# A decoder trunk whose opening is rebuilt: c loaded by columns, the first norm by a ones matrix with Ln and Exp, the first input tile in full f32, and the whole order planned anew

## The chip, the core and the metric

One core of a Trainium2 chip. The metric is the device time of one execution in microseconds (us), as a median over runs; lower is better. The engines are TensorE (PE), VectorE (DVE), ScalarE (ACT), GpSimd (POOL) and SyncE (SP, which only issues DMAs here). They run their own instruction streams in order and meet at semaphores.

## The reference

Two layers on x of 512 tokens by 1024 features. Layer 0 mixes tokens with an RG-LRU block, layer 1 with gated linear attention; a gated FFN with a causal convolution follows each. Every sub-layer has an RMS norm before it, scaled and shifted by numbers that come from a conditioning vector c, and one behind it, gated the same way.

```python
c_act = silu(c)
for i in range(2):
    mod = c_act @ ada_w[i] + ada_b[i]          # 6 x 1024 numbers
    sh_m, sc_m, gt_m, sh_f, sc_f, gt_f = split(mod, 6)
    h = rmsnorm(x, norm_g[i, 0]) * (1 + sc_m) + sh_m
    y = rglru_mixer(h, ...) if i == 0 else gla_mixer(h, ...)
    x = x + gt_m * rmsnorm(y, norm_g[i, 1])
    h = rmsnorm(x, norm_g[i, 2]) * (1 + sc_f) + sh_f
    y = conv_ffn(h, ...)
    x = x + gt_f * rmsnorm(y, norm_g[i, 3])
```

In rglru_mixer the decay is exp(-8 r softplus(-lambda)), with r a sigmoid gate of the convolved input. All in float32.

## The kernel before

**Layout.** Activations lie with features on the 128 partitions and tokens along the free axis: x is 8 tiles of 128 x 512, in two token halves of 256. Weights come in units of 128 x 1024 f32 (`in_wall_dram`, 512 KB a load). Nearly all products are split: an operand is written as a high part in the fast format fp32r and a low part, the rest, and three matmuls replace one of full f32 (`mm3`, L804: high x high, high x low, low x high). A weight's high part is a cast on ScalarE (`acopy`, L601), its low part a subtraction on DVE (`tt`, L544). For the units that `BYLOAD` (L649) names, ScalarE writes the negated tile instead and a GpSimd DMA that adds (`accum`, L637) loads the weight a second time on top of it.

**Order.** The program text only records operations. `Sched.order` (L327) is a list scheduler with costs in us per operation, a model of the DMA queues and pool sizes (3 buffers for raw weights, 3 for `araw`, 8 for `w`); it runs through the program once and fixes the order on each engine. PE and SP keep the recorded order; DVE, ACT and POOL take the ready operation with the longest tail, nudged by random numbers with one seed per section of the program (`SEEDS`, L278; six sections).

**Opening.** c comes as one row (1 x 1024) and is spread over the partitions by two matmuls with a row of ones (L865); ScalarE's Silu takes it from PSUM into `cact`. x comes in four loads, two for each token half. For each half ScalarE squares 8 pieces, DVE adds them up to two tiles, PE sums them over the partitions with one column of ones (tokens land on partitions), ScalarE divides and adds epsilon, GpSimd raises to -0.5 (`pow`, L546), and PE spreads the result with an identity matmul (`rstd_from`, L831). The second half does this in bank 5 of the eight that hold the layer's first outputs. `idle` (L860) puts helper matmuls on a column of ones between these steps.

For each input tile k = 0..7 (L1346) two tiles of the ada weights come in (`ada_col`, L1330: scale, then shift; a DVE product with `cact` that sums along the row, 128 numbers each), and one weight unit ("rgx", k). DVE and ScalarE make h[k] = x[k] rstd (1 + sc) g + sh as high and low part (`h_tile`, L931), and PE adds its product into 8 banks for the 8 output tiles. Tile 0 goes by token halves: 8 matmuls for the high and 8 for the low part of each half, then 8 of 512 tokens with the weight's low part.

**What follows.** The convolution over the 8 outputs; gate projections and block gates (`gates`, L1426: three of four blocks with raw f32 weights), a softplus of lambda on 8 columns (L1382 to L1397, some twenty small DVE operations), Tanh, Exp, Sqrt and a scan (`recur`, L1445); FFN, attention with Ln and Exp in its norm (L1724), FFN. The tail is the last down projection, its norm and the stores.

## Time and profile before

| | |
|---|---|
| median of 3 runs | 1129.67 us (1124.52 to 1132.94) |
| profiled execution | 1127.41 us |
| its span, first to last instruction | 1125.6 us |
| instructions in the span | 14788 |
| HBM read, written | 217.82 MB, 6.31 MB |
| granted TensorE clock, mean | 0.998 |

The profile is of one execution. A table by stage gives for stretches of the span the busy time of PE, PE's weight loads, DVE, ACT and POOL with the number of their instructions, the granted clock, the share of the DMA engines and GB/s. A timeline row is: start, duration, engine, line, operation, output <- inputs by buffer names, shapes, how many in a row; in brackets the idle time before it and what ended it. The name `w` is both a pool of wide buffers and what lies in them, `g` and `gh` are 512- and 256-wide working tiles, `mm` and `nr` PSUM banks, `const` tiles that stay. Matmul rows overlap, so the distance between starts is the price of one, not the duration of a row. In the profile fp32r is written f32 on PE; a matmul of true f32 runs there as two passes, each a row of its own.

### The profile page before, as it was taken

What the parts mean: (1) busy time and instruction counts of PE and PEld (TensorE: products, weight loads), DVE (VectorE), ACT (ScalarE), POOL (GpSimd) and SP (SyncE); (2) the same over time, 40 slices, a digit from 0 to 9 for tenths busy, and PEclk for the clock granted to TensorE, in tenths of its full rate; (3) what the DMA queues carried; (4) which work ended last, traced back from release to release, by engine and by line L of the source; (5) the groups of instructions that cost most, each with busy time, mean ns of one, the idle gap of its engine ahead of it and who ended that gap; (6) DMA issues with size and microseconds to landing.
All of it is one profiled execution on the core that took longest, in us unless ns stands there. A gap on an engine that the chain in (4) does not pass through costs nothing.

```text
span 1125.6 us, 14788 instructions
## 1 busy us (share of the span) xinstructions
PE 1106.1 (98%) x5293; PEld 920.1 (82%) x5293; DVE 924.6 (82%) x1573; ACT 660.0 (59%) x1028; POOL 96.0 (9%) x124
## 2 busy tenths in 40 slices
PE   7999999999999999999999999999999999999997
PEld 6775879888888888788888888889888888888886
DVE  6989899877878878799969988856877787867888
ACT  5469948657446544555896855747556444453433
POOL 1001001011110111101110100002000000000000
PEclk9999999999999999999999999999999999999999
DMA  9889776699898998884461933327386766667542
GB/s 364 295 258 306 268 236 227 154 263 294 249 268 254 251 282 220 221 241 144 132 168 57 247 110 112 113 94 237 103 241 195 176 182 157 173 146 187 150 150 75
DMA packets 64907, 225.09 MB, mean 200 GB/s; under 512 B 7233, under 2 KB 7905, under 8 KB 64834
## 3 DMA queue, kind: packets, MB, share of 16 engines
q1 hardware_dynamic: 53314, 182.73, 46.5%
q0 software_dynamic: 11520, 41.42, 20.7%
q8 instruction: 42, 0.69, 0.2%
q14 instruction: 31, 0.25, 0.1%
HBM read 217.82 MB, written 6.31 MB: 199 GB/s over the span
## 4 chain that ended last, share of the span: by engine, by line
PE 64%; DMA 12%; DVE 9%; issue 7%; ACT 6%; POOL 1%; DVEq 0%; SPq 0%; POOLq 0%; ACTq 0%
PE mm L621 63%; DMA raw<-in_wall_dram 10%; ACT g L594 3%; DVE g L558 3%; DVE w L544 2%; ACT w L601 2%; DVE w L558 1%; DVE g L544 1%; DMA w<-in_adaT_dram 1%; DMA w<-in_wall_dram 1%; DVE araw L558 1%; ACT L594 1%; PE mm L628 1%; DVE const L544 1%; ACT w L594 1%
## 5 line engine op out<-in xcount | busy, mean ns | idle before, releaser
L621 PE MATMUL mm<-g,w 128*128 128x512 f32 (+2 forms) x2758 | 615.3, 381 | 4.1 <-DMA w<-in_wall_dram 2.3
L621 PEld LDWEIGHTS mm<-g,w 128*128 128x128 f32 (+1 forms) x2758 | 501.8, 188 | 104.8 <-DMA w<-in_wall_dram 2.7
L621 PE MATMUL mm<-w,g 128*128 128x512 f32 (+1 forms) x1428 | 330.4, 389 | 0.2 <-DVE w L544 0.2
L621 PEld LDWEIGHTS mm<-w,g 128*128 128x128 f32 x1428 | 265.4, 188 | 55.4 <-DVE w L544 0.6
L601 ACT CAST w<-raw 128x1024 fp32r<-128x1024 f32 x206 | 212.7, 1040 | 163.8 <-DMA raw<-in_wall_dram 134.8
L544 DVE TENSOR_TENSOR w<-raw,w 128x1024 fp32r<-128x1024 f32 x172 | 205.6, 1208 | 53.5 <-ACT w L601 51.2
L558 DVE SCALAR_TENSOR_TENSOR g<-mm,const,g 128x510 f32<-128x510 f32 (+3 forms) x199 | 147.5, 747 | 66.5 <-ACT g L594 63.9
L544 DVE TENSOR_TENSOR g<-g,g 128x256 f32<-128x256 f32 (+3 forms) x251 | 134.7, 563 | 21.1 <-ACT g L594 11.4
L594 ACT ACTIVATE g<-mm,const 128x512 f32<-128x512 f32 x115 | 86.1, 758 | 53.3 <-PE mm L621 51.3
L594 ACT ACTIVATE g<-g 128x512 f32<-128x512 f32 (+1 forms) x136 | 69.7, 543 | 46.3 <-DVE g L558 35.6
L558 DVE SCALAR_TENSOR_TENSOR araw<-araw,const 128x1024 f32<-128x1024 f32 x72 | 86.4, 1218 | 1.4 <-DMA araw<-in_adaT_dram 1.3
L601 ACT CAST g<-g 128x512 fp32r<-128x512 f32 (+2 forms) x84 | 50.2, 603 | 51.9 <-DVE g L544 50.8
L621 PE MATMUL mm<-g,g 128*128 128x256 f32 (+3 forms) x508 | 78.1, 309 | 0.8 <-DVE g L544 0.8
L621 PEld LDWEIGHTS mm<-g,g 128*128 128x128 f32 (+1 forms) x508 | 70.5, 191 | 6.2 <-DVE g L544 1.0
L637 POOL DMA_DIRECT2D raw<-in_wall_dram x46 | 39.8, 865 | 305.4 <-ACT raw L594 98.2
L637 POOL DMA_DIRECT2D w<-in_wall_dram x34 | 29.7, 873 | 353.9 <-ACT w L594 236.3
L544 DVE TENSOR_TENSOR const<-const,mm 128x512 f32<-128x512 f32 (+1 forms) x81 | 52.6, 674 | 4.6 <-PE mm L621 4.3
L594 ACT ACTIVATE w<-raw 128x1024 fp32r<-128x1024 f32 x34 | 36.0, 1058 | 13.9 <-DMA raw<-in_wall_dram 13.9
L594 ACT ACTIVATE g<-mm 128x512 f32<-128x512 f32 x44 | 26.1, 597 | 30.0 <-PE mm L621 16.5
L594 ACT ACTIVATE g<-const 128x512 f32<-128x512 f32 x47 | 29.0, 630 | 24.6 <-DVE const L544 11.7
L549 POOL TENSOR_TENSOR sm<-sm,const 128x1 f32<-128x1 f32 (+1 forms) x26 | 21.7, 834 | 229.2 <-DVE sm L558 205.2
L594 ACT ACT_TABLE_LOAD x29 | 37.2, 1283 | 3.0 <-DVE sm L569 1.8
(119 smaller groups left out, 747.3 us busy)
## 6 DMA issues: line engine op xcount, KB each, us to landing
raw<-in_wall_dram SPq DMA_DIRECT2D x218, 512.0 KB, 4.5
araw<-in_adaT_dram SPq DMA_DIRECT2D x72, 512.0 KB, 6.1
raw<-in_wall_dram POOLq DMA_DIRECT2D x44, 512.0 KB, 7.7
w<-in_wall_dram POOLq DMA_DIRECT2D x34, 512.0 KB, 8.4
w<-in_adaT_dram SPq DMA_DIRECT2D x24, 512.0 KB, 8.1
g<-dram SPq DMA_DIRECT2D x24, 256.0 KB, 5.7
dram<-const SPq DMA_DIRECT2D x8, 512.0 KB, 2.9
const<-in_xT_dram SPq DMA_DIRECT2D x4, 512.0 KB, 5.0
```

The source lines that it names most:

```text
L544: self.s.add(eng, dur, lambda: e.tensor_tensor(out.ap(), a.ap(), b.ap(), op=op), [a, b], [out])
L549: lambda: self.nc.gpsimd.tensor_tensor(out.ap(), a.ap(), b.ap(), op=ALU.pow), [a, b], [out])
L558: return self.nc.vector.scalar_tensor_tensor(out.ap(), a.ap(), f(sc), b.ap(), op0=op0, op1=op1, **kw)
L594: return self.nc.scalar.activation(out.ap(), a.ap(), func, **kw)
L601: self.s.add("act", (0.095 if self._sb(a) else 0.052) + out.n * 0.8325e-3, lambda: self.nc.scalar.copy(out.ap(), a.ap()), [a], [out], afte ...
L621: r.append(self.nc.tensor.matmul(g[0].ap(), g[1].ap(), g[2].ap(), start=g[3], stop=g[4], **kw))
L628: self.s.add("pe", 0.112, lambda: self.nc.tensor.transpose(out.ap(), a.ap(), ident.ap()), [a, ident], [out])
L637: self.s.add("pool", 0.9, lambda: self.nc.gpsimd.dma_start(out.ap(), src, accum_op=ALU.add), [out], [out], xfer=nbytes)
```

## The change

- c is loaded as 128 x 8 columns, and Silu is taken of these 8 columns; PE spreads each over the partitions by an identity matmul, and ScalarE copies the 1024 numbers out. The identity is loaded second, the parameters between the two halves of x.
- The first norm: squares and fewer DVE sums (2 in the first half, 1 in the second), then a full 128 x 128 matrix of ones on PE sums over partitions and spreads at once, in a bank of its own; ScalarE takes Ln and Exp(-0.5 ...). An explicit table load (natural log and exp in one set) stands ahead of the squares. `rstd_from` and `rstd_bcast` are gone.
- Input tile 0: its weight is kept as loaded, h tile 0 is kept in f32, and 16 matmuls of full f32 (8 for each token half) replace 32 + 8 split ones. Its high and low parts are made later, for the gate projections.
- Ada tiles of the shift part go to the pool `araw`, those of the scale part stay in `w`. Helper matmuls: `WARM` from (3, 2, 2, 2) to six ahead of all, then 0, 0, 2, 2.
- The softplus goes from DVE to GpSimd, its reciprocal by a power of -1.
- `BYLOAD` keeps only the odd units of the first up-projection: 9 of 18 make their low part on DVE now. ScalarE makes 9 negated copies fewer.
- Ln and Exp of the attention norm ask for the common table.
- The planner: new seeds in five of six sections, the cost of a GpSimd DMA 0.8 later when both queues are busy, PE warm at 7 us instead of 20.

```diff
-WARM_AT = 20.0
+HWR = 400e3
+WARM_AT = 7.0
-DMA_HW, DMA_SW = (393e3, 132e3, 1.63, 1.11, 0.34), (220e3, 123.5e3, 1.74, 1.85, 0.0)
+PRELOAD = {"lnexp": "natural_log_exp_and_others"}
+DMA_HW, DMA_SW = (HWR, 132e3, 1.63, 1.11, 0.34), (220e3, 123.5e3, 1.74, 1.85, 0.8)
...
-SEEDS, NUDGE = (9127, 7551, 2985, 6212, 7264, 540), 0.5
+SEEDS, NUDGE = (8506, 9486, 8142, 394, 6073, 540), 0.5
...
-BYLOAD = lambda what, *i: what in ('rgg', 'gv') or what == 'up' and i[0] == 0 and i[1] >= KF and 4 <= i[1] - KF
-WARM = (3, 2, 2, 2)
+BYLOAD = lambda what, *i: what in ('rgg', 'gv') or what == 'up' and i[0] == 0 and i[1] >= KF and 4 <= i[1] - KF and i[1] % 2
+WARM = (0, 0, 2, 2, 6)
+COLRING = "araw", "w"
+SQADD = 2, 1
...
-    e.load(crow[0:D].rows(1), c_d, 4096)
-    for j in range(4):
+    e.load(ccol[:], c_d, P * KD * 4)
+    e.load(ident[:], ident_d, P * P * 4)
+    for j in range(2):
         e.load(xbuf[j * D:(j + 1) * D], xT[:, j * D:(j + 1) * D], P * D * 4, alone=True)
     e.load(par[0:NPAR0], par_d[:, 0:NPAR0], P * NPAR0 * 4)
-    e.load(ident[:], ident_d, P * P * 4)
+    for j in range(2, 4):
+        e.load(xbuf[j * D:(j + 1) * D], xT[:, j * D:(j + 1) * D], P * D * 4, alone=True)
...
+            if UNITS[j][0] == ("rgx", 0):
+                raw = s.buf("w", F32, 2 * D)[0:D]
+                e.load(raw, wall[j, :, :n], P * n * 4, alone=True)
+                loaded[j] = raw
+                continue
...
+    e.act(csil[:], ccol[:], AF.Silu, table=("silu",))
+    e.act(warm[:], ones[0:1], AF.Exp, table=("lnexp",), after=s.last["act"])
+    lnexp = s.last["act"]
+    idle(4)
     for i in range(2):
         pc = xps[i]
-        e.mms([(pc[:], ones[0:P].rows(1), crow[i * S:(i + 1) * S].rows(1), True, True)])
-        e.act(cact[i * S:(i + 1) * S], pc[:], AF.Silu, table=("silu",))
+        e.mms([(pc[j * P:(j + 1) * P], csil[i * 4 + j:i * 4 + j + 1].map(lambda a: a.to_broadcast([P, P]), P),
+                ident[:], True, True) for j in range(4)])
+        e.acopy(cact[i * S:(i + 1) * S], pc[:])
+        idle(i)
...
+    def first_sums(i):
+
+        sq = squares[i]
+        for j in range(SQADD[i]):
+            e.tt(sq[2 * j][:], sq[2 * j][:], sq[2 * j + 1][:], ALU.add)
+        parts = [t[c:c + SH] for j, t in enumerate(sq) if j % 2 == 0 or j >= 2 * SQADD[i] for c in (0, SH)]
+        out = nrb[i * SH:(i + 1) * SH]
+        for j, v in enumerate(parts):
+            e.mms([(out, ones[:], v, j == 0, j == len(parts) - 1, True)])
+        r = rs0[i * SH:(i + 1) * SH]
+        e.act(r, out, AF.Ln, bias=epsc[0:1], scale=1.0 / D, table=("lnexp",), after=lnexp)
+        e.act(r, r, AF.Exp, scale=-0.5, table=("lnexp",))
...
+        h0 = gt()
+        for sl in HALVES:
+            e.stt(h0[sl], x[0][sl], mcol(0, 1, 0), rs0[sl], ALU.mult, ALU.mult)
+            e.act(h0[sl], h0[sl], AF.Identity, bias=mcol(0, 0, 0))
+            for m in range(NX):
+                e.mms([(xps[m][sl], w[m * P:(m + 1) * P], h0[sl], sl is HALVES[0], False, True)])
+        e.acopy(h[0][0][:], h0[:])
+        e.tt(h[0][1][:], h0[:], h[0][0][:].f32(), ALU.subtract)
...
-    e.dve(0.12, lambda: nc.vector.reciprocal(s8[:].ap(), s8[:].ap()), [s8[:]], [s8[:]])
-    e.tt(s8[:], s8[:], e8[:], ALU.mult)
+    e.pow(s8[:], s8[:], mone[:])
+    e.tt(s8[:], s8[:], e8[:], ALU.mult, "pool")
...
     for d in (13, 11, 9, 7, 5, 3, 1):
-        e.tt(p8[:], p8[:], q8[:], ALU.mult)
-        e.ts(p8[:], p8[:], 1.0 / d, None, ALU.add)
+        e.tt(p8[:], p8[:], q8[:], ALU.mult, "pool")
+        e.ts(p8[:], p8[:], 1.0 / d, None, ALU.add, eng="pool")
...
-        e.act(rs[:], sums[:], AF.Ln, bias=epsc[0:1], scale=1.0 / 256, table=("ln",))
-        e.act(rs[:], rs[:], AF.Exp, scale=-0.5, table=("exp",))
+        e.act(rs[:], sums[:], AF.Ln, bias=epsc[0:1], scale=1.0 / 256, table=("lnexp",))
+        e.act(rs[:], rs[:], AF.Exp, scale=-0.5, table=("lnexp",))
```

What the new order makes of it, at three places (numbers behind names tell buffers apart; lines of the changed file lie 4 to 12 further down).

PE before, from the spreading of the first half's norm (`nr_155`) on: `const_88` is the helper's operand, `w_192` the high part of the first weight, `g_203` the high part of h tile 0, `sm_210` the second half's norm.

```order
L621 MATMUL nr_155<-const_105,sm_175 128x128 x2
L621 MATMUL mm_168<-const_88 128x512 x2
L621 MATMUL mm_182<-const_84,gh_170 128x1 x2
L621 MATMUL mm_168<-const_88 128x512 x2
L621 MATMUL mm_109<-g_203,w_192 128x256
L621 MATMUL mm_119<-g_203,w_192 128x256
L621 MATMUL mm_219<-g_203,w_192 128x256
L621 MATMUL mm_182<-const_105,sm_210 128x128 x2
L621 MATMUL mm_168<-const_88 128x512 x2
L621 MATMUL mm_232<-g_203,w_192 128x256
```

PE now, from its first matmul on: `const_118` is Silu of c, `nr_163` the bank of the norm, `w_129` the weight as loaded.

```order
L626 MATMUL mm_98<-const_88 128x512 x6
L626 MATMUL mm_124<-const_103,const_118 128x128 x4
L626 MATMUL mm_141<-const_103,const_118 128x128 x4
L626 MATMUL nr_163<-g_137,const_84 128x256 x2
L626 MATMUL nr_163<-g_165,const_84 128x256 x2
L626 MATMUL mm_98<-const_88 128x512 x2
L626 MATMUL nr_163<-g_171,const_84 128x256 x2
L626 MATMUL nr_163<-g_177,const_84 128x256 x2
L626 MATMUL nr_163<-g_184,const_84 128x256 x2
L626 MATMUL mm_98<-const_88 128x512 x2
L626 MATMUL mm_124<-g_203,w_129 128x256
```

Both halves' norms now stand ahead of the first matmul of the layer, where the second half's stood in the middle of the tile, and six helpers stand ahead of everything.

DVE before, from the first product with an ada tile (`w_107`, scale; `w_111`, shift) to the second half of h tile 0; `w_115` and `w_123` are the ada tiles of input tile 1.

```order
L558 SCALAR_TENSOR_TENSOR w_107,const_179<-w_107,const_131 128x1024
L558 SCALAR_TENSOR_TENSOR w_111,const_179<-w_111,const_131 128x1024
L558 SCALAR_TENSOR_TENSOR gh_195<-const_98,const_186,nr_155 128x256
L569 TENSOR_SCALAR g_203<-gh_195,const_186 128x256
L558 SCALAR_TENSOR_TENSOR w_115,const_179<-w_115,const_131 128x1024
L558 SCALAR_TENSOR_TENSOR g_214<-gh_195,const_186,g_203 128x256
L544 TENSOR_TENSOR w_192<-raw_113,w_192 128x1024
L558 SCALAR_TENSOR_TENSOR gh_227<-const_98,const_186,mm_182 128x256
L558 SCALAR_TENSOR_TENSOR w_123,const_179<-w_123,const_131 128x1024
```

DVE now, from the same product (`w_116`, scale; `araw_122`, shift) to the last piece of input tile 1 (`g_249`); `g_182` is the norm, `g_203` h tile 0.

```order
L562 SCALAR_TENSOR_TENSOR w_116,const_187<-w_116,const_152 128x1024
L562 SCALAR_TENSOR_TENSOR const_193<-const_187,const_110,const_161 128x1
L562 SCALAR_TENSOR_TENSOR araw_122,const_187<-araw_122,const_152 128x1024
L562 SCALAR_TENSOR_TENSOR g_203<-const_106,const_193,g_182 128x256
L548 TENSOR_TENSOR const_193<-const_187,const_110 128x1
L562 SCALAR_TENSOR_TENSOR g_203<-const_106,const_193,g_182 128x256
L562 SCALAR_TENSOR_TENSOR w_131,const_187<-w_131,const_152 128x1024
L548 TENSOR_TENSOR g_219<-g_203,g_215 128x512
L562 SCALAR_TENSOR_TENSOR araw_135,const_187<-araw_135,const_152 128x1024
L562 SCALAR_TENSOR_TENSOR g_235<-const_106,const_193,g_182 128x512
L548 TENSOR_TENSOR w_223<-raw_133,w_223 128x1024
L562 SCALAR_TENSOR_TENSOR g_249<-g_235,const_193,g_242 128x512
```

The two columns of tile 0 are made on DVE, both halves of h follow each other, and the split of the first weight is gone.

POOL before, its first rows behind the memsets: the library load, the two powers of the first norm, the power of the softplus, the first accumulating DMA.

```order
L549 ISA
L549 TENSOR_TENSOR sm_175<-sm_172,const_90 128x2
L549 TENSOR_TENSOR sm_210<-sm_207,const_90 128x2
L549 TENSOR_TENSOR const_324<-const_92,const_321 128x8
L637 DMA w_499<-in_wall_dram 128x1024
```

POOL now, from the first accumulating DMA on (`w_451`, gate projection 0).

```order
L642 DMA w_451<-in_wall_dram 128x1024
L553 ISA
L553 TENSOR_TENSOR const_510<-const_90,const_504 128x8
L574 TENSOR_SCALAR const_522<-const_510 128x8
L553 TENSOR_TENSOR const_522<-const_522,const_92 128x8
L548 TENSOR_TENSOR const_522<-const_522,const_510 128x8
L548 TENSOR_TENSOR const_551<-const_522 128x8
L574 TENSOR_SCALAR const_553<-const_551 128x8
L548 TENSOR_TENSOR const_553<-const_553,const_551 128x8
```

The library load has moved behind the first DMA, and the softplus follows it: 23 small operations and two powers up to the two columns that Exp and Tanh read, with the DMA of gate projection 1 (`w_549`) after the tenth small one.

## The prediction, made before the changed kernel ran

> **What bounds the kernel now.** I read the page's busy table first, then the table by stage, then the timeline of the opening, engine by engine.

> ```profile
> PE 1106.1 (98%) x5293; PEld 920.1 (82%) x5293; DVE 924.6 (82%) x1573; ACT 660.0 (59%) x1028; POOL 96.0 (9%) x124
> 0.00:15.50 15.50, 10.37 (x31) 7.25 (x32) 8.07 (x17) 9.16 (x18) 1.50 (x9) 1.00 0.87 329
> ...
> 62.70:111.60 48.90, 47.80 (x170) 31.36 (x168) 44.76 (x76) 42.10 (x56) 4.47 (x7) 1.00 0.89 269
> ...
> 200.00:500.00 300.00, 297.72 (x1329) 247.16 (x1328) 241.36 (x377) 162.03 (x210) 35.44 (x41) 0.99 0.89 250
> 500.00:800.00 300.00, 297.46 (x1669) 256.96 (x1668) 248.25 (x492) 204.52 (x379) 24.59 (x35) 1.00 0.46 139
> ...
> 1100.00:1125.60 25.60, 19.24 (x97) 16.24 (x95) 21.13 (x43) 8.87 (x24) 0.00 (x0) 0.97 0.22 83
> ```

> In the stage rows the second number is PE's busy time. TensorE is the bound: out of a span of 1125.6 us it idles 19.5. Of these, 15.5 - 10.37 = 5.1 lie before the first matmul of the layer and 25.6 - 19.24 = 6.4 in the tail, which the change doesn't touch; 8.0 are left between. So whatever the new order does behind the opening, it can win at most 8.0 us. The opening is the other place: until 15.5 PE does nothing that the result needs but helpers, so an earlier first matmul is a gain in full.

> ```profile
> 8.87 1.86 PE L621 MATMUL nr<-const,gh 128*128 128x1 f32 x8 [2.85 <-DVE gh L544]
> 14.99 0.68 PE L621 MATMUL mm<-const 128*128 128x512 f32 x2
> 15.51 0.51 PE L621 MATMUL mm<-g,w 128*128 128x256 f32 x3
> 16.76 0.71 PE L621 MATMUL mm<-const,sm 128*128 128x128 f32 x4 [0.74 <-POOL sm L549]
> 18.54 0.50 PE L621 MATMUL mm<-g,w 128*128 128x256 f32 x2 [0.39 <-ACT g L601]
> 23.71 4.92 PE L621 MATMUL mm<-g,w 128*128 128x512 f32 x21
> 29.15 5.21 PE L621 MATMUL mm<-g,w 128*128 128x512 f32 x21
> 35.59 4.87 PE L621 MATMUL mm<-g,w 128*128 128x512 f32 x20 [0.28 <-DVE g L558]
> 62.73 5.60 PE L621 MATMUL mm<-g,w 128*128 128x512 f32 x24
> ```

> The first input tile (32 half-wide and 8 full matmuls) runs from 15.51 to 23.71 and is torn twice by the norm of the second token half: PE stands behind GpSimd's power (16.76) and behind ScalarE's copy out of the bank that the norm shares with an output (18.54). The later tiles take 29.15 - 23.71 = 5.44 us each; seven of them would take 38.1, and 62.73 - 23.71 = 39.0 pass, so 0.9 is lost there.

> **Opening: first matmul.** What feeds it:

> ```profile
> 8.07 0.75 DVE L544 TENSOR_TENSOR gh<-g 128x256 f32<-128x256 f32 x2
> 11.57 1.22 DVE L558 SCALAR_TENSOR_TENSOR w<-w,const 128x1024 f32<-128x1024 f32 x1
> 13.38 1.05 ACT L601 CAST w<-raw 128x1024 fp32r<-128x1024 f32 x1 [0.16 <-DMA raw<-in_wall_dram]
> 14.04 0.48 DVE L558 SCALAR_TENSOR_TENSOR gh<-const,const,nr 128x256 f32<-128x256 f32 x1
> 14.55 0.37 ACT L601 COPY g<-nr 128x256 f32<-128x256 f32 x1
> 15.94 1.05 ACT L601 CAST w<-raw 128x1024 fp32r<-128x1024 f32 x1 [0.52 <-DMA raw<-in_wall_dram]
> ```

> Two 512 KB loads lie between the casts at 13.38 and 15.94, so one takes 1.28. Counted back, the two ada tiles that x needs land at about 10.7 and 11.9, and the first weight at 13.2. The change keeps that order of bytes. It drops the weight's cast and the split of the first h half. DVE has 3 instead of 8 reductions of squares ahead of the ada products, so these no longer wait for DVE but for their loads: product 10.8 to 12.0, column 0.17, second product to 13.4, h half 0.48, the other column 0.17, ScalarE's shift about 0.45 (its 256-wide copy takes 0.37, and here a bias is read too): 14.5, and first matmul at 14.7. The first half's norm must be there by 13.4. It now goes ones matmul, Ln, Exp. In the old kernel the squares of the first half were summed by 8.07 + 0.75 = 8.8 and the reciprocal root left GpSimd at 11.26 + 0.98 = 12.2 (row below). The new chain has 4 matmuls and two 256-wide activations at 0.4 each, queued on ScalarE behind three squares of 0.6: near 12. Bounds: 13.8, if the products come 0.9 sooner, and 16.0, if the extra table load and the squares behind it delay the norm by that load's 1.28:

> ```profile
> L594 ACT ACT_TABLE_LOAD x29 | 37.2, 1283 | 3.0 <-DVE sm L569 1.8
> ```

> **Opening: first tile in f32.** A matmul of true f32 runs as two passes. Their price is in the gate stage, sixteen 512-wide passes from 105.11 to 111.58:

> ```profile
> 91.37 7.03 PE L621 MATMUL mm<-g,raw 128*128 128x512 f32 x16
> 99.50 5.78 PE L621 MATMUL mm<-g,w 128*128 128x512 f32 x24 [1.10 <-ACT g L594]
> 105.11 7.03 PE L621 MATMUL mm<-g,raw 128*128 128x512 f32 x16
> 111.58 18.71 PE L621 MATMUL mm<-g,w 128*128 128x512 f32 x80
> ```

> That is 0.404 a pass, 0.202 at half width, and 16 matmuls x 2 x 0.202 = 6.5 us. Nothing tears it: bank and norm are no longer shared, and the second half of h is ready 0.6 after the first. So 14.7 + 6.5 = 21.2. The second tile needs its ada tile of the shift part, which lands at 13.2 + 3 x 1.28 = 17.1, then on DVE 1.15 + 0.67 + 1.14 + 0.67 by the rows of the old tiles, 20.8. I take 21.4 for its start against 23.71: **-2.3** (bounds -3.3 and +1.0). Then DVE needs 1.15 + 1.15 + 0.67 + 1.14 + 0.67 = 4.8 per tile against PE's 5.44, and by SP's order a weight more is under way ahead of the ring of three: of the 0.9 lost I take back 0.5: **-0.5** (0 to -0.9).

> **Softplus on GpSimd.** The chain on 8 columns leaves DVE, where its steps take 0.17 to 0.20, and goes to GpSimd, 23 small operations and two powers; the library's load (ISA) that stood ahead of the first norm now stands ahead of it, and a weight's accumulating DMA in its middle.

> ```profile
> 11.26 0.98 POOL L549 TENSOR_TENSOR sm<-sm,const 128x2 f32<-128x2 f32 x1 [10.20 <-ACT sm L594]
> 27.09 1.64 POOL L549 TENSOR_TENSOR const<-const,const 128x8 f32<-128x8 f32 x1 [10.38 <-DVE const L544]
> 50.07 1.06 POOL L637 DMA_DIRECT2D w<-in_wall_dram  x1 [21.35 <-DVE g L558]
> 54.65 0.20 DVE L1386 RECIPROCAL const<-const 128x8 f32<-128x8 f32 x1
> 82.84 1.27 ACT L594 ACTIVATE g<-mm,const 128x512 f32<-128x512 f32 x2 [1.55 <-DVE const L569]
> 85.42 3.23 ACT L594 ACTIVATE g<-g,const 128x512 f32<-128x512 f32 x4
> 0.74 0.32 POOL L645 MEMSET const<- 128x128 f32 x4 [0.29 <-POOLq L1824]
> ```

> No row has such an operation on GpSimd: below is a memset's 0.1, above the power on 8 columns, 1.64. I take 0.4, nearer the memset, since one multiplication is less than a power. The library load lasts at most 10.2 (the old gap from 1.06 to 11.26); I take half, 5. The first weight's DMA, which leaves GpSimd at 51.1 in the old trace, stands ahead of both and comes some 1 to 2 sooner; the chain then starts near 55 and ends at 55 + 2 x 1.64 + 23 x 0.4 + 0.9 = 68. The first Exp on ScalarE reads it. Gates of block 0 start on PE at 65.5 now, two groups of 1.6 each, then Tanh and a table load: 71. In the old trace ScalarE met its first Exp only at 85.42, after a wait for the DVE chain. So the wait goes and ScalarE starts earlier on the stretch in which PE waits for it (the sixteen passes from 91.37 end at 97.8, the next matmul is at 99.50: 1.7 lost); one more table load there, 1.28, takes part of it back: **-0.5** (bounds -1.7 and the late chain among the rivals).

> [...]

> **Fewer accumulating loads.** Of 18 units of the first up-projection that made their low part by an accumulating DMA, the nine even ones go back to DVE. The largest single stall of the trace hangs on an even one, number 40 (counted through GpSimd's DMAs in program order):

> ```profile
> 453.64 1.06 ACT L594 ACTIVATE w<-raw 128x1024 fp32r<-128x1024 f32 x1 [0.57 <-DMA raw<-in_wall_dram]
> 454.99 0.86 POOL L637 DMA_DIRECT2D w<-in_wall_dram  x1 [12.28 <-ACT w L594]
> 455.78 6.06 PE L621 MATMUL mm<-g,w 128*128 128x512 f32 x26
> 464.12 2.45 PE L621 MATMUL mm<-g,w 128*128 128x512 f32 x7 [2.28 <-DMA w<-in_wall_dram]
> ```

> Its raw tile is there at 453.6, when ScalarE makes the negated copy that the DMA then adds to. Without the copy, the cast (1.05) and a DVE subtraction of 1.22 end before 457, ahead of 461.8, when PE stops: **-2.3** (bounds -2.3 and 0). The nine subtractions are 11 us of DVE in a stage in which it idles 300 - 241 = 59, and ScalarE gets nine copies of 1.06 back. Without that room they would cost up to their 11.

> **The rest.** In the second mixer Ln and Exp share one table; by the new order 8 loads become 7, with one more at the start and one more in the gate stage: nothing, and the table does what the change says: in the new order Exp follows Ln with no load between. The planner's new seeds move everything up to the last half of the second FFN. Of the remaining idle time (300 - 297.5 = 2.5 between 500 and 800 is the most of it) any part may go, and new stalls like those found here, 0.3 to 2.3, may come; one of them, **+1** (bounds -3 and +5). Sum: -2.3 - 0.5 - 0.5 - 2.3 + 1.0 = -4.6, a span of 1121.0. The profiled execution took 1127.4 with its 1.8 around the span, the median of the three runs is 1129.7, 2.3 above it; so 1125.1 for the median.

> **The rivals.** (A) The GpSimd chain is late: **slower**. ScalarE takes its instructions in order, and behind the Exp that waits stand the cast of the next gate block and the emptying of PSUM. ScalarE idles 48.9 - 42.1 = 6.8 in that stage, so it decides from about 6.8 + 4.6 = 11 late, that is a chain to 82 and (82 - 59) / 23 = 1.0 per operation; at 1.64 it ends at 97, 26 late, and PE loses 19: 1125.1 + 0.5 + 19 = 1145. For it: powers alone show 0.98 on two columns. Against: the cost of a power is the function. (B) PE comes cold into the first tile. The helper matmuls show the clock although the granted clock says 1.00 all along: two 512-wide ones at 14.99 end in 0.68, while

> ```profile
> 10.60 1.63 PE L621 MATMUL mm<-const 128*128 128x512 f32 x3
> 2.28 3.75 PE L621 MATMUL mm<-araw,const 1*128 1x512 f32 x4 [2.28 <-DMA araw<-in_c_dram]
> ```

> three take 1.63, 0.43 apart, and a pass of f32 0.94. The new opening has six helpers at once from about 1.3 and little between 7 and 14. If that leaves the clock low, the tile costs up to 6.5 more: 1125.1 + 6.5 = 1131.6, and half of it 1128. [...] (C) The gain of 4.6 is given back by the next waits or by new stalls, each of the size found here: 1129.7, no change. For it: the first tiles leave DVE 0.6 of slack each, and ScalarE is busy in 42.1 of the 48.9 us of the gate stage; against: from 200 to 500, on the same feeds, PE idles 2.3 in 300 us, and that is the one stall named above. (D) The new order also clears 4 of the stalls left: 1121. For it: none of them is a full engine, each is one late piece; against: they hang on code that is not changed.

> **How the numbers follow.** Forecast 0.55, A 0.1, B 0.1, C 0.15, D 0.1. The runs before differ by up to 0.7%, and about 1%, 11.3 us, is what a measurement of this kernel can tell from no change. Faster by over 1% would need 1118.4, more than all the idle time that the change reaches can well give (2.3 + 0.9 + 8.0, less what tears the first tile, 1.1): 0.04. Slower by over 1%, above 1141, is the far half of A and a mishap of the replanning: 0.06. Within 1%: 0.9. For 8 in 10 the range goes from 1118, D with the lower bounds of the opening, to 1132, which holds B and C; the forecast alone has 1121 to 1129.

> **What would show it.** First matmul of the layer at 14.7, f32 and 6.5 long without a gap; second tile at 21.4, the first gate projection (62.73 before) at about 60. GpSimd's small operations near 0.4, the last before 71, no wait of ScalarE on GpSimd. No PE wait for an accumulating weight between 200 and 500. Wrong, if the second tile starts after 23, if PE idles more than 8 us between first matmul and tail, or if GpSimd's operations cost a microsecond.

## The result, and the profile after

The changed kernel takes 1120.78 us (median of 17 runs, 1119.49 to 1122.02), the kernel before 1126.42 in the same session (17 runs, 1123.12 to 1132.94): a ratio of 0.9947, 95% interval 0.9934 to 0.9959. Of the two profiled executions the span went from 1125.6 to 1118.4, so **7.2 us** are to be found in the trace. From the page of after, busy time, granted clock and the chain that ended last:

```profile
span 1118.4 us, 14761 instructions
PE 1105.2 (99%) x5294; PEld 920.8 (82%) x5294; DVE 930.2 (83%) x1552; ACT 659.6 (59%) x1022; POOL 98.7 (9%) x138
PEclk9999999999999999999999999999999999999999
PE 95%; DVE 1%; DMA 1%; ACT 1%; issue 0%; SPq 0%; POOL 0%; DVEq 0%; ACTq 0%; POOLq 0%
```

PE is busy for 1105.2 us (1106.1 before); what went is mostly waiting. The chain is 95% PE (64% before): almost nothing is left that releases PE late. By like matmuls, the lead over before grows like this:

| place | before | after | lead, us |
|---|---|---|---|
| second tile starts | 23.71 | 22.36 | 1.35 |
| first gate projection | 62.73 | 60.65 | 2.08 |
| the 96 matmuls that end the gate stage | 111.58 | 108.08 | 3.50 |
| first 256-wide matmuls behind the gate stage | 180.06 | 176.20 | 3.86 |
| last matmul ahead of the wait at 462 | 461.45 | 457.58 | 3.87 |
| first matmul behind it | 464.12 | 457.80 | 6.3 |
| 22 matmuls later | 470.87 | 462.79 | 8.1 |
| second mixer, behind 560 | 568.83 | 561.75 | 7.1 |
| end | 1125.6 | 1118.4 | 7.2 |

The opening on PE, timeline of after; the columns are start, duration, instruction, count and the wait ahead of it:

```profile
1.26 2.93 PE L626 MATMUL mm<-const 128*128 128x512 f32 x6 [1.26 <-DVE const L574]
3.98 3.36 PE L626 MATMUL mm<-const,const 128*128 128x128 f32 x16
...
11.27 2.86 PE L626 MATMUL nr<-g,const 128*128 128x256 f32 x12 [0.55 <-ACT g L599]
13.77 0.79 PE L626 MATMUL mm<-const 128*128 128x512 f32 x2
15.54 3.29 PE L626 MATMUL mm<-g,w 128*128 128x256 f32 x14 [0.98 <-ACT g L599]
...
22.11 0.59 PE L626 MATMUL nr<-g,w 128*128 128x256 f32 x2
```

The f32 tile is unbroken and 6.8 long (15.54 to 22.36), but its first matmul comes at 15.54, not earlier than the 15.51 of before. What it waits for stands on ScalarE and VectorE, timelines of after:

```profile
14.16 0.47 ACT L599 ACTIVATE g<-nr,const 128x256 f32<-128x256 f32 x1 [2.13 <-PE nr L626]
14.67 0.42 ACT L599 ACTIVATE g<-g 128x256 f32<-128x256 f32 x1
14.99 0.49 ACT L599 ACTIVATE g<-g,const 128x256 f32<-128x256 f32 x1
```

```profile
11.65 1.23 DVE L562 SCALAR_TENSOR_TENSOR w<-w,const 128x1024 f32<-128x1024 f32 x1 [0.86 <-DMA w<-in_adaT_dram]
14.20 0.48 DVE L562 SCALAR_TENSOR_TENSOR g<-const,const,g 128x256 f32<-128x256 f32 x1
```

The first ada weights arrive late for VectorE (its product starts at 11.65, where the prediction had 10.8), so the first half of h stands at 14.7; and ScalarE, in order, does Ln (14.16) and Exp (14.67) of the second half before the shift of the first half (14.99) that PE waits for.

The gate stage (from the first gate projection to the 96 matmuls) has no PE wait left; timelines of after, PE and ScalarE:

```profile
60.65 5.60 PE L626 MATMUL mm<-g,w 128*128 128x512 f32 x24
66.09 7.03 PE L626 MATMUL mm<-g,raw 128*128 128x512 f32 x16
72.56 16.90 PE L626 MATMUL mm<-g,w 128*128 128x512 f32 x72
...
108.08 22.34 PE L626 MATMUL mm<-g,w 128*128 128x512 f32 x96
```

```profile
71.25 1.28 ACT L599 ACT_TABLE_LOAD   x1
72.55 1.73 ACT L599 ACTIVATE g<-g,const 128x512 f32<-128x512 f32 x2
```

The first Exp starts at 72.55; in before it came at 85.42.

In the first FFN the wait for an accumulated weight is gone, and with it something that the prediction had not priced. Columns of the windows view: window, length, busy time (and instructions) of PE, PE's weight loads, VectorE, ScalarE and GpSimd, granted clock, DMA share, GB/s. First after, then before in four pieces: the wait, and what follows it.

```profile
200.00:500.00 300.00, 300.00 (x1333) 248.68 (x1332) 258.91 (x391) 158.49 (x205) 27.76 (x32) 1.00 0.83 235
```

```profile
461.84:464.12 2.28, 0.00 (x1) 0.01 (x1) 1.92 (x5) 0.00 (x0) 0.00 (x0) 1.00 1.06 246
464.12:465.20 1.08, 1.08 (x5) 0.90 (x6) 0.00 (x0) 0.92 (x1) 0.00 (x0) 1.00 1.05 250
465.20:468.60 3.40, 3.40 (x10) 2.64 (x9) 1.47 (x2) 1.97 (x5) 0.00 (x0) 0.50 0.67 192
468.60:470.00 1.40, 1.40 (x8) 1.13 (x7) 1.40 (x2) 1.40 (x3) 0.12 (x1) 0.99 0.62 252
```

One microsecond after PE resumes, the granted clock is 0.50 for 3.4 us. The 22 matmuls from 464.12 to 470.87 take 6.75 where 22 x 0.226 = 5.0 is usual: the wait of 2.28 cost 4.2 in all, by the leads (8.08 - 3.87). One new wait came in, in the second mixer:

```profile
560.74 1.17 PE L626 MATMUL mm<-g,g 96*128 96x512 f32 x4 [0.78 <-DVE g L548]
```

### The profile page after: what moved, and what is told of

The parts are those of the page before. It is cut to its first block, busy times and chain, and to the rows that moved or that the text cites. A ratio compares the mean times of both kernels' runs of the same rounds, so it can differ in the third digit from the quotient of the medians.

```text
span 1118.4 us, 14761 instructions
## 1 busy us (share of the span) xinstructions
PE 1105.2 (99%) x5294; PEld 920.8 (82%) x5294; DVE 930.2 (83%) x1552; ACT 659.6 (59%) x1022; POOL 98.7 (9%) x138
## 3 DMA queue, kind: packets, MB, share of 16 engines
q1 hardware_dynamic: 53456, 182.73, 47.4%
HBM read 213.10 MB, written 6.31 MB: 196 GB/s over the span
## 4 chain that ended last, share of the span: by engine, by line
PE 95%; DVE 1%; DMA 1%; ACT 1%; issue 0%; SPq 0%; POOL 0%; DVEq 0%; ACTq 0%; POOLq 0%
PE mm L626 94%; PE nr L626 1%; PE mm L633 1%; DMA const<-in_xT_dram 1%; DMA raw<-in_wall_dram 1%; ACT g L599 0%; DVE g L548 0%; DVE const L548 0%; ACT gh L599 0%; DVE g L562 0%; SPq L637 0%; DVE const L562 0%; POOL sm L553 0%; ACT g L606 0%; DVE w L548 0%
## 5 line engine op out<-in xcount | busy, mean ns | idle before, releaser
L626 PE MATMUL mm<-g,w 128*128 128x512 f32 (+3 forms) x2751 | 613.6, 381 | 1.0 <-ACT g L599 1.0
L548 DVE TENSOR_TENSOR w<-raw,w 128x1024 fp32r<-128x1024 f32 (+2 forms) x180 | 215.2, 1209 | 29.7 <-ACT w L606 29.5
L562 DVE SCALAR_TENSOR_TENSOR araw<-araw,const 128x1024 f32<-128x1024 f32 x80 | 96.5, 1219 | 9.2 <-DMA araw<-in_adaT_dram 9.2
L606 ACT CAST g<-g 128x512 fp32r<-128x512 f32 (+1 forms) x85 | 49.8, 603 | 46.7 <-DVE g L548 45.6
L548 DVE TENSOR_TENSOR const<-const,mm 128x512 f32<-128x512 f32 (+1 forms) x81 | 53.9, 677 | 13.4 <-PE mm L626 13.4
L642 POOL DMA_DIRECT2D w<-in_wall_dram x25 | 21.9, 875 | 299.6 <-ACT w L599 279.9
L548 DVE TENSOR_TENSOR g<-g,mm 128x512 f32<-128x512 f32 x48 | 32.4, 684 | 11.7 <-PE mm L626 11.6
L553 POOL TENSOR_TENSOR sm<-sm,const 128x1 f32<-128x1 f32 x24 | 20.3, 851 | 207.8 <-DVE sm L562 195.7
L599 ACT ACTIVATE w<-raw 128x1024 fp32r<-128x1024 f32 x25 | 26.5, 1059 | 14.7 <-DMA raw<-in_wall_dram 11.9
```

The lines of the kernel that those rows point to most:

```text
L548: self.s.add(eng, dur, lambda: e.tensor_tensor(out.ap(), a.ap(), b.ap(), op=op), [a, b], [out])
L553: lambda: self.nc.gpsimd.tensor_tensor(out.ap(), a.ap(), b.ap(), op=ALU.pow), [a, b], [out])
L562: return self.nc.vector.scalar_tensor_tensor(out.ap(), a.ap(), f(sc), b.ap(), op0=op0, op1=op1, **kw)
L599: return self.nc.scalar.activation(out.ap(), a.ap(), func, **kw)
L606: self.s.add("act", (0.095 if self._sb(a) else 0.052) + out.n * 0.8325e-3, lambda: self.nc.scalar.copy(out.ap(), a.ap()), [a], [out], afte ...
L626: r.append(self.nc.tensor.matmul(g[0].ap(), g[1].ap(), g[2].ap(), start=g[3], stop=g[4], **kw))
```

## The experiments

Two questions. Does each edit bring what the trace shows at its place? And is it the edit that brings it, or the order that the planner drew with new seeds? Every edit makes the planner draw anew, so each kernel below differs from its parent in more than its edit. Ratios are to the kernel before, timed on the same chip; the median of before was 1126.7 in the first set of four, 1128.1 in the second, 1127.3 in the third. So two kernels of different sets are compared by their ratios (0.1% is 1.1 us), not by their times.

**One part at a time, on the kernel before.** Accumulating loads alone (e1):

```diff
-BYLOAD = lambda what, *i: ... and 4 <= i[1] - KF
+BYLOAD = lambda what, *i: ... and 4 <= i[1] - KF and i[1] % 2
```

> The kernel before with one edit: of the eighteen units of the first up-projection whose low part an accumulating DMA makes, the nine even ones are made by VectorE instead. Theory (the wait at 462 and what follows it): the 2.28 us in which TensorE waits for an accumulated weight go, and so do the 22 slow matmuls behind it (0.307 us each against 0.226, 1.8 us): 4.1 us less, a span near 1121.5 and a ratio near 0.9964, and the granted clock stays at 1.00 between 460 and 470. Rival 1 (the new seeds of the planner bring the gain): no change, within 1 us. Rival 2 (the slow matmuls have another cause than the idle ahead of them): 2.3 us less, and the granted clock is still low between 464 and 470.

1132.19 us, ratio 1.0054 [1.0034, 1.0075]: slower. The place behaves as the theory says: PE is busy in 300.0 of the 300 us from 200 to 500. But the new order has other waits: 0.98 at 30, 1.17 at 529, 1.42 at 546, and these, from its table of waits:

```profile
PE mm L621 <- DVE araw L544: 2.2, 1, 2.2
PE mm L621 <- DVE g L544: 1.7, 1, 1.7
```

The 2.2 is at 702.9 and is again followed by 3.4 us at a clock of 0.50. Neither the theory's 4.1 less nor "no change" came: a saving in one place was more than lost in others.

Seeds and DMA constants alone (e2):

```diff
-WARM_AT = 20.0
+WARM_AT = 7.0
-DMA_HW, DMA_SW = (393e3, ...), (..., 0.0)
-SEEDS, NUDGE = (9127, 7551, 2985, 6212, 7264, 540), 0.5
+DMA_HW, DMA_SW = (400e3, ...), (..., 0.8)
+SEEDS, NUDGE = (8506, 9486, 8142, 394, 6073, 540), 0.5
```

> The kernel before with the planner's new constants alone: the new seeds, the new rate and setup of the DMA queues, the new point from which helper matmuls are counted. What is computed where stays as before. Theory: no gain, between -2 and +2 us, the wait of TensorE for an accumulated weight near 460 stays within 1 us of its 2.28, and the opening stays (first matmul near 15.5, second tile near 23.7). Rival (the gain is one of planning): 3 us less or more, most of it near 460.

1132.23 us, ratio 1.0053 [1.0032, 1.0074]. The rival falls: planning alone brings no gain. The theory's "no change" falls as well: these seeds cost this program 6 us, the second tile starts at 25.07, and a wait of 2.08 for ScalarE at 150 is followed by half clock. The wait for a weight, at 468, is 0.33, not 2.28, with the same eighteen accumulating loads.

The opening alone (e3; in the changed kernel, all else set back, the seeds, DMA constants and tables of the second mixer too; only `WARM_AT` stays at 7.0):

```diff
-BYLOAD = lambda what, *i: ... and 4 <= i[1] - KF and i[1] % 2
+BYLOAD = lambda what, *i: ... and 4 <= i[1] - KF
-    e.ts(s8[:], e8[:], 2.0, None, ALU.add, eng="pool")
+    e.ts(s8[:], e8[:], 2.0, None, ALU.add)
...
```

> The changed kernel with the accumulating loads, the softplus on VectorE, the activation tables of the second mixer and the planner's seeds and DMA constants of before: the opening alone is new. Theory: the second tile starts near 22.4 against 23.7 and the first gate projection near 60.7 against 62.7 (2.1 us less), the gate stage does not gain the further 1.4, and the wait near 460 stays with its slow matmuls; the time is 1 to 3 us less than that of the kernel before, a ratio of 0.998. Rival 1 (the opening is worth nothing by itself, its gain came with the new seeds): the first gate projection starts after 62. Rival 2 (the opening also brings the gate stage's gain, since it has ScalarE and VectorE ahead of their work there): the shift against before at 108 to 131 us is 3.5.

1129.05 us, ratio 1.0029 [1.0015, 1.0043]: slower. The first gate projection comes at 61.55 (62.73 before), so the opening's gain is there, and the first rival falls; then PE waits 1.46 and 3.65 for ScalarE in the gate stage (at 109 and 115), and 3.4 us of half clock follow. The 96 matmuls start at 114.92, 3.3 later than before: the second rival falls, the gate stage's gain is not the opening's. One part of the theory fails too: the wait near 460 does not stay, although all eighteen units accumulate (0.55 at 475 and 0.74 at 493, both on VectorE, are what is there).

The softplus on GpSimd alone (e4):

```diff
-    e.ts(s8[:], e8[:], 2.0, None, ALU.add)
+    e.ts(s8[:], e8[:], 2.0, None, ALU.add, eng="pool")
...
```

> The kernel before with the softplus chain on GpSimd alone. Theory: TensorE's gate stage gains 1 to 1.5 us (the 96 matmuls that started at 111.58 start near 110.3, in which the first Exp no longer waits for VectorE's chain), the wait near 460 stays, and the time is about 1 us less. Rival (the gate stage's gain came with the opening, VectorE being ahead): no gain in that stage, within 0.3 us. Rival 2 (the GpSimd chain is late when VectorE's statistics are as late as before): ScalarE waits on GpSimd before its first Exp and the stage loses 1 us or more.

1127.17 us, ratio 1.0011 [0.9994, 1.0028]: no difference that can be measured. The gate stage gains what was expected, 1.2 (62.71 to 110.37 is 47.66; before 48.85), with no PE wait. The wait of 2.28 at 464 is gone (0.31, on VectorE at 470, is all that is left there) although all eighteen units accumulate; a wait of 2.60 for ScalarE at 530.7 takes its place, with half clock behind it.

**Taken out of the changed kernel.** From these four the theory was formed anew: each edit saves at its place, and the order that is drawn with it costs some microseconds elsewhere unless its seeds were chosen for it. Softplus back on VectorE (e5):

```diff
-    e.ts(s8[:], e8[:], 2.0, None, ALU.add, eng="pool")
+    e.ts(s8[:], e8[:], 2.0, None, ALU.add)
...
```

> The changed kernel with the softplus chain on VectorE again, and its seeds kept. Theory: TensorE's gate stage, from the first gate projection to the 96 matmuls that end it, takes 1.2 us longer than the 47.4 of the changed kernel, because the first Exp waits for VectorE again; with what the new order costs elsewhere, 1 to 9 us more in all, 1122 to 1130. Rival (VectorE is ahead through the new opening, so that GpSimd is not needed): the gate stage stays within 0.3 us of 47.4.

1133.44 us, ratio 1.0045 [1.0030, 1.0059], by the ratios 11 us above the changed kernel. The direction is the theory's, the size is not: PE loses 8.5 to ScalarE in the gate stage, not 1.2, and has the half clock twice. The stage takes 59.15 instead of 47.43, which is 11.7 of the 13.1 by which the span is longer. Timeline of PE:

```profile
92.66 3.70 PE L626 MATMUL mm<-g,raw 128*128 128x512 f32 x8 [1.39 <-ACT g L599]
96.58 1.98 PE L626 MATMUL mm<-g,raw 128*128 128x512 f32 x4 [0.22 <-ACT g L599]
...
111.69 3.68 PE L626 MATMUL mm<-g,raw 128*128 128x512 f32 x4 [2.49 <-ACT g L599]
119.74 5.49 PE L626 MATMUL mm<-g,w 128*128 128x512 f32 x12 [4.37 <-ACT g L599]
```

All eighteen accumulating loads again (e7):

```diff
-BYLOAD = lambda what, *i: ... and 4 <= i[1] - KF and i[1] % 2
+BYLOAD = lambda what, *i: ... and 4 <= i[1] - KF
```

> The changed kernel with all eighteen units loaded by the accumulating DMA again, and its seeds kept. Theory: TensorE waits again between 455 and 490 for a weight, 0.3 to 2.3 us, as in all three kernels with the eighteen units that have run beside the kernel before; with 1.7 us more of half clock if it is 2 us or more; in all 0.5 to 5 us more than the changed kernel, 1121 to 1126. Rival (the new seeds have removed that wait): no wait above 0.2 us between 455 and 490.

1121.77 us, ratio 0.9948 [0.9929, 0.9967], the changed kernel's own is 0.9947. The rival holds: there is no wait in the FFN, eighteen accumulating loads or nine.

```profile
200.00:500.00 300.00, 300.00 (x1333) 248.68 (x1332) 247.76 (x379) 162.96 (x211) 35.49 (x41) 1.00 0.87 247
```

**The same seeds for both kernels.** Only the line SEEDS differs from the parent. The seeds of before in the changed kernel (e8):

```diff
-SEEDS, NUDGE = (8506, 9486, 8142, 394, 6073, 540), 0.5
+SEEDS, NUDGE = (9127, 7551, 2985, 6212, 7264, 540), 0.5
```

> The changed kernel with the planner's seeds of before; all else is as changed. The four kernels so far that took over one part of the change each were not faster. Theory, formed anew from them: each edit saves what it saves at its own place, and every edit makes the planner draw a new order, which elsewhere costs 3 to 9 us of new waits unless the seeds were chosen for it; a wait of 2 us or more is followed by 3.4 us at half clock, 1.7 us more. So here: first gate projection between 60 and 62, no wait for a weight between 200 and 500 above 0.5 us, and in all 3 to 9 us more than the changed kernel, 1124 to 1130. Rival (the edits carry the gain whatever the seeds): within 1.5 us of the changed kernel, 1119.5 to 1122.

The seeds 1 to 6 in the changed kernel (e10) and in the kernel before (e11):

```diff
+SEEDS, NUDGE = (1, 2, 3, 4, 5, 6), 0.5
```

> The changed kernel with the seeds 1 to 6, which nobody chose. Theory (every order not chosen for its program costs 3 to 9 us of waits): 1124 to 1130, with waits that lie elsewhere than those of the last kernel. Rival (the edits carry the gain whatever the seeds): 1119.5 to 1122.

> The kernel before with the seeds 1 to 6, which nobody chose; to be set against the changed kernel with the same seeds (1130.2). Theory (the opening and the softplus on GpSimd save 3 to 5 us with any seeds; the draw of the order adds 0 to 10 to either kernel): 1130 to 1140, with the first gate projection after 62 and the first Exp of the gate stage after 80, against 60.0 to 61.4 and 72.5 in every changed kernel that has the softplus on GpSimd. Rival (the whole difference between the two kernels is one of seeds): 1125 to 1130, not slower than the changed kernel with the same seeds.

The seeds 11 to 16 in the changed kernel (e12) and in the kernel before (e13):

```diff
+SEEDS, NUDGE = (11, 12, 13, 14, 15, 16), 0.5
```

> The changed kernel with the seeds 11 to 16. Theory: 1121 to 1131, first gate projection between 60 and 62 and first Exp near 72.5. Every wait of TensorE of 2.1 us or more, and none of 1.2 us or less, is followed within 3.4 us by a stretch of about 3.4 us in which the granted clock is 0.50, which costs 1.7 us. Rival (seeds alone): not faster than the kernel before with these seeds.

> The kernel before with the seeds 11 to 16. Theory: 1126 to 1138, and 3 us or more above the changed kernel with these seeds. Rival (seeds alone): not slower than the changed kernel with these seeds.

| seeds | program of before | changed program | difference of the ratios |
|---|---|---|---|
| those of before | 1 (1126.4) | 0.9967 [0.9949, 0.9985] (1123.4) | -0.3% |
| those of after | 1.0053 [1.0032, 1.0074] (1132.2; with the constants) | 0.9947 [0.9934, 0.9959] (1120.8) | -1.1% |
| 1 to 6 | 1.0090 [1.0070, 1.0109] (1137.2) | 1.0022 [1.0003, 1.0040] (1130.2) | -0.7% |
| 11 to 16 | 1.0119 [1.0101, 1.0137] (1141.0) | 1.0019 [1.0007, 1.0031] (1129.0) | -1.0% |

"Seeds alone" falls, as far as four pairs can show it: with each of the four sets the changed program is faster, by 4 to 12 us. The same seeds are not the same draw, since the programs differ, so each row sets two draws side by side; but leaving out each program's own seeds, the slowest changed one (1.0022) is still ahead of the fastest of before (1.0053). And "the edits carry it whatever the seeds" falls too: with other seeds the changed program takes, by the ratios, 2.3, 8.1 and 8.5 us more, so two of three such draws are slower than the kernel before. Each program is fastest with its own seeds; how these were found is not on record. Four details of the expectations failed: the changed program with the seeds of before lost 2.3, below the 3 to 9 expected; e10, at 1130.2, lies just above its range and e13, at 1141.0, 3 us above; and the first Exp of the program of before with seeds 1 to 6 came at 75.07, not after 80. What was expected of the clock held in e12: a wait of 2.38 at 545 had the half clock, the others, 1.37 and less, had not.

What is common to one side of the table lies in the first 130 us. The first gate projection starts between 60.6 and 61.6 in all eight kernels with the new opening and between 62.7 and 64.3 in all six with the old. In the gate stage PE waits for ScalarE, in the seven kernels with the softplus on VectorE, 1.10, 0.56, 0, 5.1, 8.5, 6.9 and 7.5 us; in the seven with it on GpSimd 0, six times, and 0.28. The 0 is e2, and it shows that a late chain is not the whole cause. Timeline of its PE:

```profile
64.25 5.60 PE L621 MATMUL mm<-g,w 128*128 128x512 f32 x24
...
105.21 7.03 PE L621 MATMUL mm<-g,raw 128*128 128x512 f32 x16
111.68 1.71 PE L621 MATMUL mm<-g,w 128*128 128x512 f32 x5
```

With the softplus on VectorE its stage takes 47.43 us all the same, and its first Exp comes at 75.41. In the four kernels that lose 5 us or more, ScalarE waits for VectorE 1.4 us at most in the whole stage (1.21 in e5, at 79.92); beside that stand late weights (a wait of 3.24 in e5, 2.77 in e13) and eight or nine table loads in the stage, where the seven kernels with GpSimd have seven. So with the softplus on GpSimd the stage loses 0.3 at most to ScalarE, seven times of seven; that the chain on VectorE by itself holds PE for 5 us is not shown.

**Helper matmuls away (e9).**

```diff
-WARM = (0, 0, 2, 2, 6)
+WARM = (0, 0, 0, 0, 0)
```

> The changed kernel without the ten helper matmuls of the opening. Theory (the clock is granted by how busy TensorE has been; the transposes and the 128x256 sums alone do not keep it up): part of the first tile runs at half rate, 0.43 to 0.46 us a matmul of 128x256 in f32 against 0.22, for 3.4 us or more, and the second tile starts 1.7 to 3.5 us later than 22.36. Rival (the transposes and sums warm it by themselves): the first tile lasts 6.8 as in the changed kernel.

A single run of 1128.48. The question was the first tile, and the rival holds: with the transposes and sums alone ahead of it the tile runs at full rate, 0.21 a pass, and lasts 6.82 (15.95 to 22.77). Timeline of PE:

```profile
11.68 2.86 PE L626 MATMUL nr<-g,const 128*128 128x256 f32 x12 [0.83 <-ACT g L599]
15.95 3.29 PE L626 MATMUL mm<-g,w 128*128 128x256 f32 x14 [1.41 <-ACT g L599]
...
22.53 0.59 PE L626 MATMUL nr<-g,w 128*128 128x256 f32 x2
22.77 5.15 PE L626 MATMUL mm<-g,w 128*128 128x512 f32 x21
```

The first rise of the granted clock on record is at 7.79, ahead of the tile (6.93 in the changed kernel). The rest of its time is waits of another order (1.94 at 151, 1.47 at 172, 1.06 at 569).

## Why the prediction was right, and where it was wrong

The forecast was a span of 1121.0, a median of 1125.1 and "within 1%"; they came to 1118.4, 1120.8 and 0.5%. The likeliest case was the right one, but in part by luck: the largest gain came for another reason than the one given, and one term too large stands against others too small. The forecast put the median 4.1 above the span, from three runs of before (1129.7); seventeen runs have theirs at 1126.4, and in after the median is 2.4 above the span. By its terms:

- **First tile, -2.3: -1.35.** The f32 tile was sized well (6.8 for 6.5). The step that failed is the start of its first matmul, put at 14.7 and measured at 15.54: the first product waits for its load until 11.65 instead of 10.8, and that ScalarE takes Ln and Exp of the second half ahead of the shift of the first had not been read out of the new order (0.3: the half of h stands at 14.68, the shift starts at 14.99).
- **K loop, -0.5: -0.73.** Right.
- **Softplus, -0.5: -1.42.** The wait goes as forecast (first Exp at 72.55 for a forecast of 71, no wait of ScalarE on GpSimd); e4 alone shows 1.2 in that stage. The size was too small: all that PE lost at 99.50 went, 1.4, and the table load that was taken off the gain cost PE nothing (the stage has seven instead of four). The trace of before could not show that the same stage loses 5 to 8.5 in other orders, nor, as e2 does, 0 in one. Of the two edits that were taken out of the changed kernel singly, this is the one that it can't do without, with its seeds.
- **Accumulating loads, -2.3: 4.2 went at that place, and not by this edit.** Two steps failed. The price left out the half clock behind the wait, 1.8. And the cause: the wait belonged to one drawn order. It vanished with eighteen accumulating loads as well (none in e7, 0.33 in e2, 0.31 and on VectorE in e4, 0.55 and on VectorE in e3), and the time of e7 is that of the changed kernel. The edit alone, in e1, does remove the wait, and its order loses more elsewhere. It saves 4.7 MB of HBM reads (217.82 to 213.10) and, as far as these runs show, no time.
- **New waits, +1 (bounds -3 and +5): about +0.9** from 470 to the end. The value is right, and luckily so; the bounds were too narrow: with other seeds the changed kernel loses up to 8.5 more, and the two kernels with arbitrary seeds, 1130.2 and 1129.0, are near the upper end of the range or rival C. That the changed kernel keeps its gain is the work of its seeds together with its edits; nothing in the trace of before could tell the draw.

Rival A did not come. The 23 small operations take 0.41 each on average in after, for a forecast of 0.4, and 0.83 in e4; there the whole chain of 25 takes 25.2 us, 1.0 for each, the value from which rival A was to decide, and 16.3 in after. It starts early enough (52.5 and 27.0) to end ahead of the first Exp (at 68.8 and 52.2). The library's load, put at 5, is 3.8 at most in after: so long GpSimd idles ahead of its first operation, at 52.49, and VectorE ends that wait. Rival B did not come: the tile runs at full rate, 0.21 a pass, and e9 shows that it does so without the helpers too. Its sign was read right: the clock record of before starts with the rise to 1.00 at 14.65, so the 1.00 that the views show ahead of that is no measurement, and the matmuls 0.43 apart at 10.60 are. Rival C did not come with these seeds and would have come with seeds 1 to 6 or 11 to 16. Rival D's 1121 is the measured time, but by the lower median of before and not by its cause: behind 470 nothing was cleared, 0.9 was lost. What stays open is how much of the difference at equal seeds, 4 to 12 us, is due to each edit, and to each part of the opening (its loads, its norm and its f32 tile were not run singly): the opening shows 1.3 to 3.6 at the first gate projection, the softplus 0 to 8.5 in the gate stage, and what lies behind it is not separable from the draw.

## What to carry to other kernels

In a kernel whose order a planner draws, the effect of one edit is timed under several seeds for both versions; a single pair of orders compares edits and draws together, and e1 and e3 show edits that save at their place and lose in all in the draw that came with them. The wait that a trace shows belongs to its order: before an edit is credited with it, see whether it is still there when something unrelated is changed. And a wait of PE of 2 us is priced with the slow clock that may stand behind it (1.7 us here), not by its own length.

## What the hardware did that was not expected

**Half clock behind short waits.** Ten of the fourteen traces show the same between opening and tail: a wait of PE, then 3.4 us at a granted clock of 0.50, which costs 1.7 (6.8 in e5 and e11 and 13.7 in e13, where waits of 4 us and more lie in it). Another instance, windows of the changed kernel with seeds 1 to 6:

```profile
529.69:532.06 2.37, 0.00 (x1) 0.00 (x1) 2.05 (x4) 1.39 (x4) 0.67 (x2) 0.94 0.00 0
532.06:535.40 3.34, 3.34 (x11) 2.75 (x12) 3.34 (x8) 3.03 (x7) 0.55 (x1) 0.53 0.51 164
535.40:537.00 1.60, 1.60 (x13) 1.43 (x12) 0.45 (x1) 0.15 (x2) 0.00 (x0) 1.00 0.77 261
```

```profile
461.80:465.21 3.41, 1.13 (x6) 0.92 (x6) 1.96 (x5) 0.93 (x1) 0.00 (x0) 1.00 1.08 251
555.58:558.99 3.41, 1.50 (x11) 1.25 (x10) 2.60 (x9) 3.11 (x10) 0.61 (x2) 1.00 0.14 16
147.74:151.15 3.41, 1.59 (x8) 0.97 (x6) 3.41 (x7) 0.98 (x1) 0.00 (x0) 1.00 0.94 274
```

PE idles for 2.28, 1.91 and 1.82 us of them; behind the third the clock stays. From the first rise to 1100 us of all fourteen traces, PE idles for 1.91 or more in the windows ahead of 12 of the 13 falls, and for 1.82 or less in every window at full clock with no fall behind it; the 13th fall, in e3, stands behind 1.47. The wait of 1.94 in e9, which two windows share, passed without the half clock. That the idle time in one such window decides is a reading of these records; no run isolates it.

**GpSimd's small operations took 0.2 to 1.1 us, and their time changed with what VectorE did beside them.** Timelines of after, GpSimd and then VectorE:

```profile
62.47 0.54 POOL L548 TENSOR_TENSOR const<-const,const 128x8 f32<-128x8 f32 x1
63.10 0.73 POOL L574 TENSOR_SCALAR const<-const 128x8 f32<-128x8 f32 x1
...
66.11 0.20 POOL L548 TENSOR_TENSOR const<-const,const 128x8 f32<-128x8 f32 x1
66.40 0.23 POOL L574 TENSOR_SCALAR const<-const 128x8 f32<-128x8 f32 x1
```

```profile
59.44 4.30 DVE L562 SCALAR_TENSOR_TENSOR g<-g,const,g 128x511 f32<-128x511 f32 x6
63.82 5.36 DVE L562 SCALAR_TENSOR_TENSOR g<-mm,const,g 128x511 f32<-128x511 f32 x8
```

These operations on 8 columns take 0.54 to 0.74 while VectorE works on operands in SBUF alone (six at 0.7, from 59.44), and 0.20 to 0.24 from 65.18 to 68.1, beside VectorE's operations that read one operand from PSUM (0.48 for the one at 64.62, the first beside them); two at 57.9 and 58.2, where VectorE stands idle, take 0.20 as well. In e4, where the chain runs beside VectorE's 128x1024 operations on SBUF (1.22 each), its operations take up to 1.09. What makes the difference, no run isolates.
